# Out-projection of six feature blocks as fill of a scan's last stretch, and first feed-forward products in column halves

## The chip, the cores and the metric

The kernel runs on one core of one Trainium2 chip. The metric is the device time of one execution in microseconds. TensorE multiplies, VectorE (DVE), ScalarE (ACT) and GpSimd (POOL) do the rest, SyncE (SP) and POOL issue most transfers.

## The reference, cut to what matters

Two transformer blocks on 512 tokens of 1024 features, in float32. The first block's first layer is a bidirectional RWKV-7 mixer followed by a residual sum, a layer norm and a SwiGLU feed-forward of width 2816; a pooling layer with a mixture of experts and the second block (attention and a convolutional feed-forward) come behind and aren't touched.

```python
def rwkv7_out(y, feats, r_k, g1, g2, lnx_g, lnx_b, w_o):
    ...
    yn = ((y - mean) * lax.rsqrt(var + RK_GN_EPS)).reshape(b, n, D_MODEL) * lnx_g + lnx_b
    ...
    gate = jax.nn.sigmoid(xg @ g1) @ g2
    return ((yn + bonus).astype(xg.dtype) * gate) @ w_o
```

Behind it the layer computes, with alpha = 4 ** 0.25 and gates gt1, gt2 from the adaptive modulation, x = layer_norm(alpha * x + gt1 * y), then h = x * (1 + sc2) + sh2, then swiglu(h) = (silu(h @ w1) * (h @ w3)) @ w2.

## The kernel before

**Products in parts.** A float32 product is made of three: each operand is split into a high part (a cast on ACT, L167) and a low part (the difference on DVE, L168), and mm3 (L173) issues high x high, high x low and low x high into one accumulator.

**The scan (phase_rwkv).** Eight feature blocks f of 128 features (two heads each) go one after the other through 12 steps of 64 tokens, three chain() stretches of 16 slots each, so 48 slots per block and 384 in all. A step computes Rs (ACT, L863), UV (ACT, L871) and the state S (DVE, L890), with the decayed state SP by POOL (L850) beside it. weave() runs the chain with side work: the inverses of the next tiles, gram(), features of the block after, and tail(f - 1), which normalises a finished block, adds the bonus, multiplies by the gate and writes it to DRAM (ygd, L945). The copy of a block's result out of PSUM is L899: the end of its scan.

**Background work.** background() is one generator: the jobs of the k, r and v projections of pairs p = 1 to 3 (job(), matmuls at L979), then 40 yields of adaptive modulation (ada(), matmuls at L235). fill() calls it after each slot, by the table PACE of (slot, yields done by then); all that fill() issues stands behind the chain's last matmul. A lateral job loads its left operand in pieces of 1 MB on the POOL queue (L969, tile x, two buffers) and its weights on SP (tile w). In a v job a yield is six matmuls of 256 columns.

**The order of instructions.** A scheduler orders each engine's instructions when the program is built, by a model of time and by the order of the program; an instruction of a later stage can stand ahead of one of an earlier stage if its buffers are free. Engines then run their instructions in that order.

**Behind the scan (body).** After the last slot the rest of the background is run, then tail(7), then: the eight blocks of y are read back into xres and split into y3 (two of the three buffers of the pool act), x is loaded into xres, the whole w_o is loaded and split, and for each of four token blocks tb and two column halves 24 matmuls of 512 columns are issued, resid_add() adds to xres (DVE, L1311 and L1315), and norm_tail() normalises (statistics on DVE L1130, a power on POOL L1137, the scaling on ACT L1139) and turns the block into features (transposes on PE L1162, scale and shift on ACT L1169 and DVE L1171, the split into hT). hT has two parts, in the same pool act. Then phase_ffn(): glu() for each pair of w1 and w3 columns, beside ada_sum(), which computes the next modulations on DVE (L288) from weights that it loads on SP.

## Time and profile before

| | us |
|---|---|
| time before, median of 3 runs | 3043.56 (3039.95 to 3060.38) |
| the profiled execution's own time | 3043.58 |
| its span in the trace | 3041.8 |

In that execution TensorE was busy 2665.8 us (88%), DVE 1562.1, ACT 1218.2 and POOL 826.3. A busy TensorE is not TensorE at its peak: matmuls are pipelined and their ends are modelled. Busy time tells which engine could be the limit of a stretch; the waits in the timelines tell which one is. In the rows below, an idle time in brackets is that of the engine before the instruction, and behind the arrow stands what ended it.

### The profile page before, as it was taken

What the parts mean: (1) busy time and instruction counts of PE and PEld (TensorE: products, weight loads), DVE (VectorE), ACT (ScalarE), POOL (GpSimd) and SP (SyncE); (2) the same over time, 40 slices, a digit from 0 to 9 for tenths busy, and PEclk for the clock granted to TensorE, in tenths of its full rate; (3) what the DMA queues carried; (4) which work ended last, traced back from release to release, by engine and by line L of the source; (5) the groups of instructions that cost most, each with busy time, mean ns of one, the idle gap of its engine ahead of it and who ended that gap; (6) DMA issues with size and microseconds to landing.
All of it is one profiled execution on the core that took longest, in us unless ns stands there. A gap on an engine that the chain in (4) does not pass through costs nothing. (4 is left out here: it accounts for less than half of the span.)

```text
span 3041.8 us, 49004 instructions
## 1 busy us (share of the span) xinstructions
PE 2665.8 (88%) x19592; PEld 2127.8 (70%) x19592; DVE 1562.1 (51%) x2443; ACT 1218.2 (40%) x2267; POOL 826.3 (27%) x908
## 2 busy tenths in 40 slices
PE   5878788898898766899897999999949989989999
PEld 3666677677776545677686787887837855778887
DVE  5865656756656536754446531111155467554544
ACT  5644545555555423225432321111123367342422
POOL 2453434534534321018534300000033100112120
PEclk8976788997888778999898999999979979999999
DMA  7562334544543536757622767788972212122321
GB/s 256 184 219 68 97 114 144 183 137 129 172 135 105 173 128 199 242 173 229 194 84 97 267 208 236 256 273 291 299 253 72 71 37 72 58 83 89 106 88 65
DMA packets 346594, 477.99 MB, mean 157 GB/s; under 512 B 45842, under 2 KB 242723, under 8 KB 339703
## 3 DMA queue, kind: packets, MB, share of 16 engines
q1 hardware_dynamic: 328664, 404.80, 41.2%
q0 software_dynamic: 10480, 60.31, 6.1%
q10 hardware_dynamic: 7216, 9.68, 1.0%
q8 instruction: 157, 2.57, 0.4%
q14 instruction: 77, 0.63, 0.1%
HBM read 419.34 MB, written 55.39 MB: 156 GB/s over the span
## 5 line engine op out<-in xcount | busy, mean ns | idle before, releaser
L168 DVE TENSOR_TENSOR wl<-w,wh 128x1024 fp32r<-128x1024 f32 (+1 forms) x271 | 332.1, 1232 | 473.6 <-ACT wh L167 472.4
L167 ACT CAST wh<-w 128x1024 fp32r<-128x1024 f32 (+1 forms) x271 | 256.5, 953 | 551.3 <-PE mm L173 469.3
L173 PE MATMUL mm<-act,wh 128*128 128x512 f32 x1408 | 439.6, 394 | 14.5 <-ACT act L167 14.5
L173 PEld LDWEIGHTS mm<-act,wh 128*128 128x128 f32 x1408 | 265.6, 190 | 73.7 <-ACT act L167 15.0
L173 PE MATMUL mm<-act,wl 128*128 128x512 f32 x704 | 275.5, 391 | 0.0
L173 PE MATMUL mm<-wh,act 128*128 128x512 f32 x816 | 262.0, 400 | 7.5 <-ACT wh L167 4.2
L173 PEld LDWEIGHTS mm<-wh,act 128*128 128x128 f32 x816 | 157.3, 193 | 47.0 <-ACT wh L167 7.2
L286 POOL TENSOR_TENSOR act<-act 128x512 f32<-128x512 f32 x96 | 142.7, 1491 | 139.7 <-ACT act L285 75.5
L301 POOL DMA_DIRECT2D bc<-gate x6 | 3.6, 593 | 614.4 <-DVEq L1707 523.6
L173 PE MATMUL mm<-wl,act 128*128 128x512 f32 x408 | 163.1, 400 | 2.8 <-DVE wl L168 2.8
L1220 DVE TENSOR_TENSOR silu<-silu,mm 128x512 f32<-128x512 f32 (+4 forms) x77 | 35.3, 458 | 248.3 <-PE mm L1216 183.1
L173 PEld LDWEIGHTS mm<-act,wl 128*128 128x128 f32 x704 | 133.1, 189 | 28.1
L799 DVE STREAM_TRANSPOSE XT<-T 128x512 f16<-128x512 f16 x120 | 84.6, 705 | 100.4 <-ACT T L797 100.2
L743 POOL TENSOR_TENSOR GA<-GA,masks 128x512 f32<-128x512 f32 (+1 forms) x96 | 100.1, 1053 | 103.7 <-ACT GA L742 100.5
L739 PE MATMUL gm<-kr,bk 64*128 64x128 f32 (+1 forms) x768 | 115.4, 324 | 4.2 <-ACT GA L742 2.4
L739 PEld LDWEIGHTS gm<-kr,bk 64*128 64x128 f32 x768 | 99.4, 224 | 25.2 <-ACT GA L742 9.8
L792 DVE TENSOR_TENSOR W<-pW,masks 128x512 f16<-128x512 f32 x120 | 81.9, 682 | 64.4 <-PE pW L790 63.8
L850 POOL TENSOR_TENSOR SP<-S,pc 128x64 f32<-128x64 f32 x176 | 59.2, 355 | 194.3 <-DVE S L890 183.0
L1216 PEld LDWEIGHTS mm<-moxh,w 128*128 128x128 f32 x704 | 105.0, 190 | 8.3 <-issue 5.7
L1216 PE MATMUL mm<-moxh,w 128*128 128x192 f32 (+1 forms) x704 | 108.0, 314 | 2.5 <-DMA w<-in_moe_w_dram 2.4
L797 ACT CAST T<-pT 128x512 f16<-128x512 f32 x120 | 69.7, 581 | 83.2 <-PE pT L795 79.8
L285 ACT ACTIVATE act<-act,cT 128x512 f32<-128x512 f32 x96 | 67.6, 723 | 81.6 <-DMA act<-in_w_ada_dram 81.4
(521 smaller groups left out, 6382.7 us busy)
## 6 DMA issues: line engine op xcount, KB each, us to landing
w<-in_moe_w_dram SPq DMA_DIRECT2D x109, 1024.0 KB
w<-in_ffn_w_dram SPq DMA_DIRECT2D x32, 1024.0 KB
act<-in_ada_w_dram SPq DMA_DIRECT2D x96, 256.0 KB
act<-in_w_ada_dram SPq DMA_DIRECT2D x96, 256.0 KB
w<-in_w_up_dram SPq DMA_DIRECT2D x22, 1024.0 KB
x<-xdk POOLq DMA_DIRECT2D x18, 1024.0 KB, 5.6
x<-xdv POOLq DMA_DIRECT2D x18, 1024.0 KB, 5.7
w<-in_ada_w_dram SPq DMA_DIRECT2D x32, 512.0 KB
```

Of the source, the lines that this page charges most:

```text
L167: self.nc.scalar.copy(out=hi, in_=x)
L168: self.nc.vector.tensor_tensor(out=lo, in0=x, in1=hi.bitcast(F32), op=OP.subtract)
L173: self.nc.tensor.matmul(ps, x, y, start=start and i == 0, stop=stop and i == 2, skip_group_check=True)
L285: nc.scalar.activation(out=wt, in_=wt, func=AF.Copy, scale=c)
L286: nc.gpsimd.tensor_tensor(out=acc, in0=wt, in1=acc if kk else bias, op=OP.add)
L739: nc.tensor.matmul(pss[par][:, s2, d, :nc_], bkj(d, par, j), KR[d][PR(par), j::12, :][:, :nc_ // 64, :], start=True, stop=True)
L743: nc.gpsimd.tensor_tensor(out=out, in0=out, in1=gm, op=OP.mult)
L792: nc.vector.tensor_tensor(out=W16, in0=pW, in1=lmask[:, li, None].to_broadcast(sh), op=OP.mult)
L797: nc.scalar.copy(out=T16, in_=pT)
L799: nc.vector.transpose(fl(XT), fl(T16))
L850: nc.gpsimd.tensor_tensor(out=SP[:, d], in0=S[:, d], in1=PC[d][:, j:j + 1].to_broadcast([128, 64]), op=OP.mult)
L1216: nc.tensor.matmul(ps[:, :n], w[:, kk], xT[:, kk, :n], start=(kk == 0), stop=(kk == KB - 1))
```

## The change

- tail() splits its result and writes both parts to DRAM (yparts) in place of ygd; for f = 7 three operations go from POOL to DVE.
- A fourth kind of job, "o", for four column blocks p of 256 columns: it multiplies feature blocks 0 to 5 of y with the rows of w_o, 6 x 4 x 3 matmuls of 256 columns in 12 yields; o_out() multiplies by the gate, adds alpha * x and writes the sums to DRAM (ysums). The four jobs stand at the end of background().
- PACE: the modulation's 40 yields end at slot 322 and no longer at 384, and 26 yields of the new jobs follow up to slot 384; the rest runs four yields a step within tail(7).
- body: xres is loaded with the sums; y of blocks 6 and 7 is loaded as parts into one buffer of act; two weight tiles in place of eight; six matmuls of 512 columns for each tb and column half. norm() of block tb + 1 stands before turn() of block tb.
- glu() for the first pair: columns 0 to 255 of both products, then turn(3), then columns 256 to 511.

```diff
@@ -30,7 +30,7 @@
-        (220, 137), (236, 153), (252, 161), (268, 177), (384, 217))
+        (220, 137), (236, 153), (252, 161), (268, 177), (322, 217), (384, 243))
@@ -302,7 +302,7 @@
-def phase_rwkv(k, tables, tables2, modulate, yg):
+def phase_rwkv(k, tables, tables2, modulate, yo):
@@ -312,7 +312,8 @@
-    xd = {(n_, w): k.dr.tile([128, KB, 2, w], F32, name=f"xd{n_}{w}") for n_, w in (("k", NT), ("k", NCX), ("r", NT), ("v", NT), ("v", NCX))}
+    xd = {("o", NT): yo["parts"]}
+    xd.update({(n_, w): k.dr.tile([128, KB, 2, w], F32, name=f"xd{n_}{w}") for n_, w in (("k", NT), ("k", NCX), ("r", NT), ("v", NT), ("v", NCX))})
@@ -321,7 +322,7 @@
-    W = {"r": a["rk_w_rkv"][0, 0], "k": a["rk_w_rkv"][0, 1], "v": a["rk_w_rkv"][0, 2]}
+    W = {"r": a["rk_w_rkv"][0, 0], "k": a["rk_w_rkv"][0, 1], "v": a["rk_w_rkv"][0, 2], "o": a["rk_w_o"][0]}
@@ -363,7 +364,20 @@
-    OUT = {"k": k_out, "r": r_out, "v": v_out}
+    def o_out(p, pss, lat, pool, tag, *_):
+        g = k.t(pool, [128, 512], tag=tag)[:, :256]
+        nc.sync.dma_start(out=g, in_=k.gates["0"][0][:, p * 256:(p + 1) * 256].to_broadcast([128, 256]))
+        for i, ps in enumerate(pss):
+            t = k.t(pool, [128, 512], tag=tag)
+            rows = lambda x: x[i * 256:(i + 1) * 256, p * 256:(p + 1) * 256].rearrange("(b p) n -> p b n", p=128)
+            nc.sync.dma_start(out=halves(t), in_=rows(a["x"][0]))
+            nc.vector.tensor_tensor(out=halves(ps), in0=halves(ps), in1=g[:, None, :].to_broadcast([128, 2, 256]), op=OP.mult)
+            nc.vector.scalar_tensor_tensor(out=t, in0=t, scalar=ALPHA, in1=ps, op0=OP.mult, op1=OP.add)
+            nc.sync.dma_start(out=rows(yo["sums"]), in_=halves(t))
+        return
+    OUT = {"k": k_out, "r": r_out, "v": v_out, "o": o_out}
@@ -903,14 +917,15 @@
+            eng = nc.gpsimd if f < 7 else nc.vector
-            nc.gpsimd.tensor_tensor(out=vh, in0=vh, in1=st["cf"][:, :, None].to_broadcast([128, 8, 64]), op=OP.mult)
+            eng.tensor_tensor(out=vh, in0=vh, in1=st["cf"][:, :, None].to_broadcast([128, 8, 64]), op=OP.mult)
-            nc.gpsimd.tensor_tensor(out=y3, in0=y3, in1=mean[:, :, None].to_broadcast([128, 8, 64]), op=OP.subtract)
+            eng.tensor_tensor(out=y3, in0=y3, in1=mean[:, :, None].to_broadcast([128, 8, 64]), op=OP.subtract)
@@ -921,7 +936,7 @@
-            nc.gpsimd.tensor_tensor(out=y3, in0=y3, in1=rs[:, :, None].to_broadcast([128, 8, 64]), op=OP.mult)
+            eng.tensor_tensor(out=y3, in0=y3, in1=rs[:, :, None].to_broadcast([128, 8, 64]), op=OP.mult)
@@ -942,7 +957,11 @@
-            nc.sync.dma_start(out=yg[f], in_=yn)
+            hi, lo = (k.t(bst, [128, 512], F32R, tag="st") for _ in range(2))
+            k.part_to(hi, lo, yn)
+            for i, x in enumerate((hi, lo)):
+                nc.sync.dma_start(out=yo["parts"][:, f, i], in_=x.bitcast(F32))
+            made["y", f] = True
@@ -956,11 +975,13 @@
-            acc = [ps for ps in pss] if lat and n_ != "v" else [halves(ps)[:, i] for ps in pss for i in range(2)]
-            for kk in range(KB):
+            byrow, last_ = n_ in "vo", (6 if n_ == "o" else KB) - 1
+            acc = [ps for ps in pss] if lat and not byrow else [halves(ps)[:, i] for ps in pss for i in range(2)]
+            for kk in range(last_ + 1):
+                    n4 = min(4, last_ + 1 - kk)
-                    nc.sync.dma_start(out=raw, in_=W[n_][kk * 128:(kk + 4) * 128, p * 256:(p + 1) * 256].rearrange("(k p) n -> p k n", p=128))
+                    nc.sync.dma_start(out=raw[:, :n4], in_=W[n_][kk * 128:(kk + n4) * 128, p * 256:(p + 1) * 256].rearrange("(k p) n -> p k n", p=128))
@@ -969,15 +990,15 @@
-                    if n_ == "v":
+                    if byrow:
-                    st, sp_ = kk == 0 and (one or i % 2 == 0), kk == KB - 1 and (one or i % 2 == 1)
+                    st, sp_ = kk == 0 and (one or i % 2 == 0), kk == last_ and (one or i % 2 == 1)
-                    if i % 2 == 1 or (lat and n_ != "v"):
+                    if i % 2 == 1 or (lat and not byrow):
@@ -1024,6 +1045,9 @@
+            for p in range(4):
+                assert all(made.get(("y", f)) for f in range(6))
+                yield from job("o", p, True)
@@ -1068,8 +1092,11 @@
+        for _ in tail(7):
+            for _ in range(4):
+                next(mods, None)
-        run(tail(7))
@@ -1139,7 +1166,7 @@
-def norm_tail(k, sp, psp, tb, xres, gbc, bbc, hT, scol, bcol):
+def norm_rows(k, sp, tb, xres, gbc, bbc):
@@ -1147,8 +1174,7 @@
-    if hT is not None:
-        to_feature(k, sp, psp, xh, hT, slice(tb * 128, (tb + 1) * 128), scol, bcol)
+    return xh
@@ -1198,13 +1224,22 @@
-def glu(k, psp, sp, xT, n, w1, w3, g):
+def glu(k, psp, sp, xT, n, w1, w3, g, cols=None):
-        for w in (w1, w3):
+        if cols is not None and i == 0:
+            ws = [k.part(w[:, :, :128]) for w in (w1, w3)]
+            pss = [k.t(psp, [128, 512], tag="mm") for _ in ws]
+            for cs, make in cols:
+                make()
+                for w, ps in zip(ws, pss):
+                    for kk in range(KB):
+                        k.mm3(ps[:, cs], at(w, ALL, kk), at(xT, ALL, kk, cs), kk == 0 and cs.start == 0, kk == KB - 1 and cs.stop == n)
+        for w in (w1, w3) if not pss else ():
@@ -1257,7 +1292,7 @@
-def phase_ffn(k, hT, xres, gate2, psp, sp, gp, act, side):
+def phase_ffn(k, hT, xres, gate2, psp, sp, gp, act, side, cols):
@@ -1274,7 +1309,7 @@
-            glu(k, psp, sp, hT, NT, w1, w3, out)
+            glu(k, psp, sp, hT, NT, w1, w3, out, cols if f == 0 else None)
@@ -2067,8 +2102,8 @@
-        ygd = k.dr.tile([KB, 128, NT], F32, name="ygd")
-        phase_rwkv(k, tables, tables2, modulate, ygd)
+        yo = {"parts": k.dr.tile([128, KB, 2, NT], F32, name="yparts"), "sums": k.dr.tile([NT, D], F32, name="ysums")}
+        phase_rwkv(k, tables, tables2, modulate, yo)
@@ -2087,28 +2122,32 @@
-            with tc.tile_pool(reuse_waits="tile", name="wo3", bufs=5) as wo3:
-                y3 = feat()
-                yg = xres.rearrange("p t d -> p (t d)").rearrange("p (f n) -> p f n", f=KB)
-                for f in range(KB):
-                    nc.sync.dma_start(out=yg[:, f, :], in_=ygd[f])
-                for f in range(KB):
-                    k.part_to(*at(y3, ALL, f), yg[:, f, :])
-                nc.sync.dma_start(out=xres, in_=a["x"][0].rearrange("(t p) d -> p t d", p=128))
-                ws = []
-                for i in range(4):
-                    raw = k.load_w(a["rk_w_o"][0][(i % 2) * 512:(i % 2 + 1) * 512, (i // 2) * 512:(i // 2 + 1) * 512])
-                    ws += [k.part(raw[:, 2 * q:2 * q + 2, :], wo3 if len(ws) + q < 5 else k.wq) for q in range(2)]
-                hT = None
-                for tb in range(4):
-                    for hf in range(2):
-                        ps = k.t(psp, [128, 512], tag="mm")
-                        for kk in range(KB):
-                            k.mm3(ps, at(y3, ALL, kk, slice(tb * 128, (tb + 1) * 128)), at(ws[hf * 4 + kk // 2], ALL, kk % 2), kk == 0, kk == KB - 1)
-                        resid_add(k, sp, tb, hf, ps, gate, xres)
-                    hT = hT or feat()
-                    norm_tail(k, sp, psp, tb, xres, *gb, hT, *cols)
+            raw = k.load_w(a["rk_w_o"][0][768:1024, :])
+            ws = [k.part(raw[:, :, hf * 512:(hf + 1) * 512]) for hf in range(2)]
+            y67 = k.t(act, [128, 2, 2, NT], F32R, tag="act")
+            for i in range(2):
+                nc.gpsimd.dma_start(out=y67[:, i], in_=yo["parts"][:, 6 + i])
+            nc.sync.dma_start(out=xres, in_=yo["sums"].rearrange("(t p) d -> p t d", p=128))
+            hT = feat()
+            rows_ = {}
+            def norm(tb):
+                cs = slice(tb * 128, (tb + 1) * 128)
+                for hf in range(2):
+                    ps = k.t(psp, [128, 512], tag="mm")
+                    for i in range(2):
+                        k.mm3(ps, at((y67[:, i, 0], y67[:, i, 1]), ALL, cs), at(ws[hf], ALL, i), i == 0, i == 1)
+                    resid_add(k, sp, tb, hf, ps, gate, xres, None)
+                rows_[tb] = norm_rows(k, sp, tb, xres, *gb)
+            def turn(tb):
+                to_feature(k, sp, psp, rows_[tb], hT, slice(tb * 128, (tb + 1) * 128), *cols)
+            for tb in range(4):
+                norm(tb)
+                if tb:
+                    turn(tb - 1)
+            turns = [(slice(0, 256), lambda: None), (slice(256, 512), lambda: turn(3))]
@@ -2117,7 +2156,7 @@
-                block, room = phase_ffn(k, hT, xres, gate0, psp, sp, gp, act, side)
+                block, room = phase_ffn(k, hT, xres, gate0, psp, sp, gp, act, side, turns)
```

## Rows read from the trace of the kernel before

**Rows 1.** The page's first line: span and instructions.

```profile
span 3041.8 us, 49004 instructions
```

**Rows 2.** Stretches: length, busy (count) of PE, PEld, DVE, ACT, POOL; PEclk, DMA share, GB/s.

```profile
905.00:990.00 85.00, 73.82 (x1211) 54.86 (x1210) 51.44 (x91) 44.73 (x108) 39.83 (x62) 0.84 0.42 121
...
1068.50:1084.50 16.00, 5.10 (x14) 2.44 (x14) 3.77 (x7) 3.97 (x7) 4.93 (x5) 0.50 0.93 300
1084.50:1158.70 74.20, 55.56 (x216) 44.79 (x216) 23.99 (x43) 12.99 (x19) 17.19 (x15) 0.82 0.18 60
1158.70:1181.10 22.40, 2.04 (x10) 1.60 (x9) 21.82 (x36) 10.21 (x20) 9.27 (x9) 0.57 0.87 279
1181.10:1194.50 13.40, 13.40 (x49) 10.68 (x50) 10.08 (x14) 5.28 (x6) 0.00 (x0) 0.82 0.79 258
...
1070.00:1080.00 10.00, 3.83 (x13) 2.44 (x14) 1.62 (x4) 2.87 (x5) 4.93 (x5) 0.50 1.06 330
```

**Rows 3.** Timeline of ACT at the scan's end: start us, us, instruction.

```profile
1047.20 0.27 ACT L863 COPY Rs<-ch 128x128 f32<-128x128 f32 x1 [2.07 <-PE ch L833]
1050.75 0.27 ACT L863 COPY Rs<-ch 128x128 f32<-128x128 f32 x1 [2.07 <-PE ch L833]
...
1062.06 0.26 ACT L863 COPY Rs<-ch 128x128 f32<-128x128 f32 x1
1062.21 4.83 ACT L167 CAST wh<-w 128x1024 fp32r<-128x1024 f32 x5
1067.07 0.57 ACT L871 ACTIVATE UV<-ch 64x128 f32<-64x128 f32 x2
1068.41 0.59 ACT L899 COPY yc<-y 128x512 f32<-128x512 f32 x1 [0.78 <-PE y L833]
```

**Rows 4.** Timeline of SP's queue around the scan's end.

```profile
1043.05 2.31 SPq L155 DMA_DIRECT2D w<-in_rk_w_o_dram  x4
...
1092.11 0.38 SPq L2098 DMA_DIRECT2D xres<-in_x_dram  x1
```

**Rows 5.** Timeline of PE from the out-projection to the feed-forward.

```profile
1084.56 0.80 PE L173 MATMUL mm<-wh,act 128*128 128x512 f32 x1 [3.29 <-ACT act L167]
...
1107.08 1.97 PE L1162 MATMUL mm<-ctile,rsq 128*128 128x128 f32 x8 [8.54 <-ACT rsq L1139]
...
1181.07 2.17 PE L173 MATMUL mm<-act,wh 128*128 128x512 f32 x4 [8.57 <-ACT act L167]
```

**Rows 6.** Timeline of DVE in the same stretch.

```profile
1100.68 0.69 DVE L1315 SCALAR_TENSOR_TENSOR xres<-xres,silu 128x512 f32<-128x512 f32 x1 [4.37 <-DMA xres<-in_x_dram]
...
1158.55 1.29 DVE L168 TENSOR_TENSOR act<-u,act 128x512 fp32r<-128x512 f32 x2 [0.18 <-PE mm L173]
```

**Rows 7.** Groups by line (count, busy us, mean ns) of 1158.7 to 1181.1, then 1084.5 to 1158.7.

```profile
L288 DVE SCALAR_TENSOR_TENSOR act<-act,cT 128x512 f32<-128x512 f32 x11 | 11.4, 1044 | 0.4 <-DMA act<-in_ada_w_dram 0.4
...
L168 DVE TENSOR_TENSOR act<-xres,act 128x512 fp32r<-128x512 f32 x8 | 5.3, 692 | 4.8 <-DMA ygd<-yn 3.7 <-ACT act L167 1.0
```

**Rows 8.** Timeline of PE: a yield of a v job and its successor; a modulation yield.

```profile
737.43 0.50 PE L979 MATMUL bg<-x,wh 128*128 128x256 f32 x2
...
738.25 0.41 PE L790 MATMUL pW<-T,nl 128*128 128x64 f16 x8
...
1036.83 0.64 PE L235 MATMUL bg<-w,cT 128*32 128x256 f32 x8
```

**Rows 9.** Line L899, ends of the scans of heads 4, 5, 6 (ns, then start us).

```profile
L899 ACT COPY yc<-y x1: 587/587/587, 798.0 to 798.0; 128x512 f32<-128x512 f32 x1
L899 ACT COPY yc<-y x1: 567/567/567, 905.2 to 905.2; 128x512 f32<-128x512 f32 x1
L899 ACT COPY yc<-y x1: 591/591/591, 989.7 to 989.7; 128x512 f32<-128x512 f32 x1
```

**Rows 10.** DMA issues of 300 to 1060: count, KB each, median us to landing.

```profile
x<-xdv POOLq DMA_DIRECT2D x16, 1024.0 KB, 5.5
```

**Rows 11.** Waits of POOL in 560 to 870: us in total, times, longest.

```profile
POOL x L969 <- PE bg L979: 12.4, 7, 4.9
```

## Prediction

> **What bounds the kernel now.** I read the page's span first [rows 1]: 3041.8 us. The times list the same profiled execution at 3043.58 us, and the median of the runs shown is 3043.56, so a change summed on the trace carries over to the median one to one. Then I read the table by stretches [rows 2] around the place of the diff. In the scan's stretch 905 to 990 TensorE is busy 73.8 of 85.0 us: nearly full. From the end of the scan it is not: busy 5.1 of 16.0 us in the last head's tail, 55.6 of 74.2 in the out-projection, 2.0 of 22.4 between that and the feed-forward. The first feed-forward pair of products ends at 1194.5.
>
> The timelines say what each gap waits for. Head 7's scan ends with the copy at 1068.41 [rows 3]. Its last step but one took 1050.75 to 1062.06, where the step before it took 3.55 us, and from its Rs to its UV passed 5.0 us. ScalarE stood in order behind casts of out-projection weights (five of them, 4.83 us, sit between Rs and UV); their loads had been issued at 1043.05 [rows 4]. So some 12 us of the scan's end are a wait for weights of the next stage. Out-projection starts at 1084.56 and the feed-forward at 1181.07 [rows 5]: 96.5 us for 192 products of 512 columns, with four waits for a normalised block. The reader should see why the last wait is long: the first low part of the normalised activations is written at 1158.55, right after the last product [rows 6]. It needs a buffer that the y parts hold until then, so the turning of all four blocks piles up behind it; and in that pile VectorE is busy 21.8 of 22.4 us [rows 2], 11.4 of them with eleven instructions of the next layer's modulation [rows 7].
>
> **The change, part by part.** *Out-projection out of the row.* Six of eight feature blocks leave the serial stretch; 48 of 192 products stay. That frees the buffer: y of two blocks takes one buffer, both parts of the activations have one from the start, and turning of block n can follow the norm of n+1. This is what the change can win; what follows is what it pays.
>
> *Fill in the scan.* A job of the new kind has 12 yields of six 256-column products, four jobs have 48. By the pacing table, background work stands at 217 yields after slot 384 before and at 243 after, 40 of them adaptive-modulation yields both times (now squeezed into slots 268 to 322). So 26 yields are added under heads 5, 6 and 7. Their price: a value job has the same six products, and one such yield goes from 737.43 to 738.25 [rows 8], 0.82 us at the full clock; an adaptive yield takes 0.64. From below it can be nothing: 11 us of TensorE in 905 to 990 are idle [rows 2]. From above: head 5 (about 29.5 yields by the table) took 798.0 to 905.2, head 6 (16.5) 905.2 to 989.7 [rows 9], 22.7 us for 13 yields, 1.75 us each; this holds head 7's features too, so it is a bound. 26 yields cost 0 to 46 us. I take 20, near the TensorE price (26 x 0.82 = 21): the engine is nearly full there, and the squeezed modulation yields carry neither splits nor POOL-issued loads. The splits of y move from after the scan into the tails: eight were 5.3 us of VectorE [rows 7]; seven now lie beside other heads, 1 us on the path, 0 to 5.
>
> *The stall at the end.* Eight weight tiles to split become two before the feed-forward's, and 4 MB of load become 1 MB. Of the 12 us I count 10 as gone (0 to 12): the scheduler can still put feed-forward casts early. Scan end: 1068.4 + 20 + 1 - 10 = 1079.4.
>
> *From the scan's end to the sums.* Of 48 yields about 27 are done, 21 left, woven four to a step into the tail of head 7. 21 x 0.82 = 17 us, and head 7's tail (the stretch of 16.0 us) lies under them. That tail's three operations moved from POOL to VectorE are hidden there too; without that cover they could give or take 1 us. Between jobs, the second half's row tile must wait for the gate tile's buffer (two buffers, three tiles): multiply, load of x, add, before the next job has its second accumulator. I take 4 us; bounds 0 and 7 (a 1 MB load lands in 5.5 us [rows 10], and this one is a quarter of it). After the last product: two multiplies, the load, the add, the write of the sums, 8 us (5 to 13, by the same row twice at the top). Then xres is read back in one 2 MB load: that of x was issued at 1092.11 [rows 4] and its first reader ran at 1100.68 [rows 6], 9 us. 17 + 4 + 8 + 9 = 38 us; the sums are in place at 1117.4. The 48 remaining products need only the y parts of the tail, which ends before, so they are hidden under this wait. On SP's queue the stores of sums wait for VectorE, and behind them stand the last tail's loads and its stores of parts; a delay of these by the 8 us would still be inside the wait for the sums.
>
> *From the sums to the end of the first pair.* Here VectorE sets the pace. In 1084.5 to 1181.1 it was busy 24.0 + 21.8 = 45.8 us [rows 2]; less 11.4 (modulation) and 5.3 (splits of y) [rows 7], 29 us are the four blocks with the first weight splits. Behind its last norm stand POOL, ScalarE and the transposes, of which some 3 us show: from 1100.68 to the transposes at 1107.08 one block needed 6.4 us [rows 5, 6]. Then the second column half: 48 products of 256 columns at a sixth of 0.82 us (weight load for each included, as in that row), 7 us; the first half runs before, under the last block's norm. Modulation will again sit between: I take 5 of the 11.4. 29 + 3 + 7 + 5 = 44, bounds 37 and 51. End of the pair: 1161.4, against 1194.5.
>
> The sum: 33.1 us earlier, and the rest of the kernel is the same work behind it: 3043.6 - 33.1 = 3010.5 us.
>
> **A rule that speaks against it.** The new jobs read y parts back through the POOL queue, 3 MB a job. The stretch 1070 to 1080 moved 330 GB/s at a DMA share of 1.06 [rows 2], and nothing in the trace is faster there. The Trainium skill (DMA: Bandwidth & Descriptors, Issuing engines are not separate DMA queues) says that queues issued from different engines run on the same 16 DMA engines and interleave. By that rule the re-reads and the feed-forward weights share one rate, which the trace's share of 1.06 agrees with, and the time would be that of the second rival below.
>
> **The rivals.** *Fill lands on the chain* (chance 0.15): each of the 26 yields costs the 1.75 us of the head difference. The scan's end is 46 - 20 = 26 us later, time 3037. For it: job yields bring splits on ScalarE and VectorE, the chain's own engines. Against: 13 yields' difference also holds a whole head's features.
>
> *The end is bound by DMA* (0.14): between the scan's end and the sums must move x parts 5, x rows and sums 2, y parts 1.5, out-projection and job weights 2, feed-forward weights 3, broadcasts 1.5, xres 2 MB (sizes from shapes, estimates as to what is left by then): 17 MB at 330 GB/s are 52 us instead of 38, time 3025. For it: the share of 1.06. Against: two tiles are loaded ahead and the weights may be loaded before, as the out-projection's were.
>
> *Slower: POOL's queue holds the chain* (0.06). Loads of parts are issued by POOL in order and wait for a buffer; the state's decay product L850 that each chain step needs is queued behind them. Before, POOL waited 12.4 us in 7 such waits, the longest 4.9 [rows 11], in heads with slack. If each of the 12 loads holds for 4.9 us what the path needs (the seven under heads 6 and 7 the decay product, the five after them the tail's power on POOL, L923), that is 59 us, time 3010.5 + 59 = 3069.5; slower begins at 2.8 us a load. Against: the wait's mean was 1.8 us, so 21 us and still a gain is the more likely form.
>
> *Better* (0.15): the tail's yields are not tied to the chain and drop into its gaps; nothing is left at the scan's end but the last job's output, and fill costs half. 10 us less in the scan and 10 less behind it: 2990.
>
> **How the numbers follow.** The forecast has 0.50, with its own range 2996 to 3026 (10 us of fill and 10 behind the scan either way). Faster or slower by 1% (30.4 us: under 3013, over 3074) is about what a measurement of this kernel can tell from no change. Under 3013 lie some 0.30 of the forecast's 0.50, the better case, and a tenth of the others: 0.48. Over 3074 lies at most half of the slower rival and mishaps of pacing: 0.06. Within 1%: 0.46. The range 2985 to 3045 leaves out the upper half of the slower rival, the top of the fill rival and the lower part of the better case, together under 2 in 10.
>
> **What would show it.** After: the scan's last copy near 1079 (1068 or less: fill free; 1100 and more: fill on the chain); no long step between the last Rs copies; head 7's tail with TensorE busy and at the full clock, where before 0.50 was granted [rows 2]; xres ready about 38 us behind (50 and DMA share near 1: the DMA rival); POOL waits at the load of parts short; first feed-forward product some 25 us after xres (three of four blocks of the 29 us, and 3). I am wrong if head 6 or 7 grows by over 25 us, or if VectorE blocks after xres on modulation loads for over 15 us.

## The result, and the profile after

The changed kernel takes 3065.84 us (median of 18 runs, 3047.6 to 3074.28) beside 3041.74 for the kernel before on the same chip: the ratio is 1.0076, 95% interval 1.0062 to 1.0089. The forecast was 3010.5 us, a ratio of 0.989, within 2985 to 3045 us; the time lies above that range. The profiled execution took 3058.1 us.

The page's first line, to set beside [rows 1]:

```profile
span 3056.3 us, 49525 instructions
```

Some words stand for marks in the traces. "After" is the changed kernel, and "head n" is the scan of feature block n, from the end of the block before to its own copy out of PSUM. The first sum in xres is resid_add()'s first addition on VectorE. The first silu on ScalarE marks the end of the first feed-forward pair's products, and each pair leaves one cast of its gated product, gh; the 21st gh cast serves as a late mark.

The stretches of after, cut where the sum was cut: head 6, head 7, from the scan's end to the first sum in xres, from there to the first silu, and what follows. Columns as in [rows 2].

```profile
916.30:1013.00 96.70, 88.51 (x1339) 64.41 (x1338) 60.84 (x103) 46.96 (x111) 44.08 (x66) 0.86 0.55 167
1013.00:1092.40 79.40, 64.37 (x987) 53.11 (x986) 39.54 (x77) 34.71 (x85) 22.24 (x45) 0.87 0.70 226
1092.40:1152.80 60.40, 31.63 (x149) 27.56 (x150) 14.40 (x24) 6.44 (x11) 7.06 (x11) 0.72 0.61 204
1152.80:1218.50 65.70, 30.57 (x165) 27.47 (x164) 55.60 (x81) 22.25 (x35) 28.48 (x24) 0.69 0.47 148
1218.50:1545.00 326.50, 292.09 (x1282) 235.63 (x1281) 179.84 (x218) 128.65 (x173) 123.51 (x84) 0.94 0.65 208
```

| term of the sum, us | forecast | after | difference |
|---|---|---|---|
| scan's end | 1079.4 | 1092.4 | +13.0 |
| from there to the sums in xres | 38 | 60.4 | +22.4 |
| from there to the end of the first pair | 44 | 65.7 | +21.7 |
| from there to the end of the span (before: 3041.8 - 1193.5 = 1848.3) | 1848.3 | 1837.8 | -10.5 |

The first three make 57.1 us. Less 10.5, and with 1.0 added because the prediction took the end of the pair before as 1194.5 where this cut has 1193.5, that is the 47.6 by which the span of 3056.3 misses 3008.7. The fourth is no gain that I can name: from the 21st gh cast of the feed-forward to the end, that stretch takes 1468 to 1479 us in before, after and the kernels below (e12 aside), 1467.8 in after.

The second row is the surprise. Neither TensorE (31.63 of 60.40 us) nor VectorE (14.40) is busy in it, and the DMA share is 0.61 at 204 GB/s, so the second rival's bound (the 330 GB/s of [rows 2]) doesn't account for it either. The timeline of the last tail's result, block 7's y, on its way to the out-projection:

```profile
1108.59 0.69 DVE L959 TENSOR_TENSOR yn<-yn,gm 128x512 f32<-128x512 f32 x1 [0.45 <-PE gm L958]
...
1131.13 0.62 ACT L167 CAST st<-yn 128x512 fp32r<-128x512 f32 x1 [14.41 <-DMA ysums<-st]
...
1136.23 0.69 DVE L168 TENSOR_TENSOR st<-yn,st 128x512 fp32r<-128x512 f32 x1 [3.84 <-DMA ysums<-st]
...
1136.96 0.33 SPq L963 DMA_DIRECT2D yparts<-st  x1
...
1145.22 0.54 POOL L2130 DMA_DIRECT2D act<-yparts  x1 [24.47 <-DMA yparts<-st]
...
1149.19 0.79 PE L173 MATMUL mm<-wh,act 128*128 128x512 f32 x1 [13.41 <-DMA act<-yparts]
```

The value is ready at 1109.3, and its high part is written 22 us later. What released the cast is the landing of a store of *sums* (ysums) out of a tile called st. The tail takes the tiles for its two parts from the pool that the jobs use, which has two buffers, and each new job takes three there: gate rows, x rows, x rows. The parts queue behind the jobs' stores and loads; the store of the parts, their load back by POOL and the products follow one after another.

### The profile page after: what moved, and what is told of

Read it like the earlier page. It is cut to its first block, busy times and chain, and to the rows that moved or that the text cites. A ratio compares the mean times of both kernels' runs of the same rounds, so it can differ in the third digit from the quotient of the medians.

```text
span 3056.3 us, 49525 instructions
## 1 busy us (share of the span) xinstructions
PE 2668.5 (87%) x19784; PEld 2136.1 (70%) x19784; DVE 1581.8 (52%) x2468; ACT 1219.1 (40%) x2273; POOL 844.0 (28%) x919
## 5 line engine op out<-in xcount | busy, mean ns | idle before, releaser
L168 DVE TENSOR_TENSOR wl<-w,wh 128x1024 fp32r<-128x1024 f32 (+1 forms) x277 | 333.3, 1209 | 490.2 <-ACT wh L167 488.8
L173 PE MATMUL mm<-act,wh 128*128 128x512 f32 (+1 forms) x1440 | 444.0, 391 | 18.8 <-ACT act L167 15.0
L173 PEld LDWEIGHTS mm<-act,wh 128*128 128x128 f32 x1440 | 271.9, 192 | 76.3 <-ACT act L167 15.4
L173 PE MATMUL mm<-act,wl 128*128 128x512 f32 (+1 forms) x720 | 279.4, 388 | 0.0
L173 PE MATMUL mm<-wh,act 128*128 128x512 f32 x720 | 231.0, 400 | 22.0 <-DMA act<-yparts 17.7
L173 PEld LDWEIGHTS mm<-wh,act 128*128 128x128 f32 x720 | 138.5, 193 | 56.3 <-DMA act<-yparts 18.5
L173 PE MATMUL mm<-wl,act 128*128 128x512 f32 x360 | 143.7, 400 | 3.0 <-DVE wl L168 2.9
L1000 PE MATMUL bg<-wh,x 128*128 128x256 f32 x480 | 129.2, 338 | 13.0 <-DMA x<-yparts 13.0
L864 POOL TENSOR_TENSOR SP<-S,pc 128x64 f32<-128x64 f32 x176 | 66.7, 396 | 202.2 <-DVE S L904 192.4
L1251 PEld LDWEIGHTS mm<-moxh,w 128*128 128x128 f32 x704 | 105.0, 190 | 7.3 <-issue 6.3
L1000 PEld LDWEIGHTS bg<-wh,x 128*128 128x128 f32 x480 | 95.0, 223 | 21.5 <-issue 8.9
```

Of the source, the lines that this page charges most:

```text
L168: self.nc.vector.tensor_tensor(out=lo, in0=x, in1=hi.bitcast(F32), op=OP.subtract)
L173: self.nc.tensor.matmul(ps, x, y, start=start and i == 0, stop=stop and i == 2, skip_group_check=True)
L864: nc.gpsimd.tensor_tensor(out=SP[:, d], in0=S[:, d], in1=PC[d][:, j:j + 1].to_broadcast([128, 64]), op=OP.mult)
L1000: m = nc.tensor.matmul(o, y, z, start=st and q == 0, stop=sp_ and q == 2, skip_group_check=True)
L1251: nc.tensor.matmul(ps[:, :n], w[:, kk], xT[:, kk, :n], start=(kk == 0), stop=(kk == KB - 1))
```

## The experiments

Ratios are against the kernel before, measured on the same chip; a run's milestones come from its own profiled execution. How far these scatter is seen in e7, e9, e11, e13 and e16, which differ only behind the scan: head 0 ends at 338.5 to 351.7 us, head 5 takes 110.1 to 117.0, head 6 100.0 to 105.0, head 7 80.3 to 87.0. So I compare lengths of heads and distances behind the scan's end, not absolute times. Each version has one trace, and a head's length that differs by less than this scatter shows nothing.

**e1: the parts in buffers of their own.**

```diff
-            hi, lo = (k.t(bst, [128, 512], F32R, tag="st") for _ in range(2))
+            hi, lo = (k.t(tp1, [128, 512], F32R, tag=t_) for t_ in ("vtok", "yc"))
```

> The two parts that each tail writes get buffers of their own kind (those of vtok and yc, which the same tail has done with) in place of the two that the jobs' rows and gates also use. Theory 'buffers': in the changed kernel the cast of the last tail's result waited 14.4 us for a store of sums, from 1109.3 to 1131.1, and heads 3 to 5 grew by 11 us with the same waits; so the last parts leave near 1110, the second load of y parts no longer starts at 1145, and heads 3 to 5 go back: 8 to 18 us faster than the changed kernel (3048 to 3058). Rival 'fill': the loss is the new jobs' work itself on the chain, whatever buffer the parts lie in: within 3 us of the changed kernel.

3044.68 us, ratio 1.0017 (1.0001 to 1.0034): about 0.6%, 18 us, of the loss is this. The same timeline:

```profile
1108.19 0.69 DVE L959 TENSOR_TENSOR yn<-yn,gm 128x512 f32<-128x512 f32 x1
...
1108.96 0.62 ACT L167 CAST vtok<-yn 128x512 fp32r<-128x512 f32 x1 [2.45 <-issue]
...
1111.04 0.69 DVE L168 TENSOR_TENSOR yc<-yn,vtok 128x512 fp32r<-128x512 f32 x1
...
1126.67 0.50 PE L173 MATMUL mm<-wh,act 128*128 128x512 f32 x1 [1.68 <-DMA act<-yparts]
```

The cast follows the result at once. Now the products stand behind the last product of the new jobs (1124.7), the first sum waits 8.6 us for the load of xres, and it comes 48.6 us behind the scan's end in place of 60.4. Head 3 is back too: 108.0 us, against 117.9 in after and 108.0 before; tails inside the scan had queued for the same two buffers. But the scan as a whole isn't shorter: heads 1 to 7 take 748.8 us in e1, 741.2 in after and 718.1 before, since every other head is longer in e1 than in after, by 1 to 5 us.

**e5: the gate rows in a buffer of their own as well.**

```diff
-        g = k.t(pool, [128, 512], tag=tag)[:, :256]
+        g = k.t(tp1, [128, 256], tag="ast")
```

> As the run with own buffers for the tails' parts, and the gate tile of a new job lies in the buffer of the modulation's rows (done by then), so that the job's two row tiles no longer wait for it. If the bubble between jobs that I put at 4 us, and the load of the second half's rows after the last product, are on the path: 3 to 8 us faster than the run with own buffers alone (3037 to 3042). If the loads of y parts set the pace behind the scan, the bubble lies under them: within 3 us.

3035.99 us, ratio 0.9994 (0.9964 to 1.0024). The first sum comes 41.0 us behind the scan's end, 7.6 less than in e1. Not all of that is the wait for the gate tile: 96 matmuls of the new jobs (16.0 yields) are left behind the scan's end, where after and e1 have 113 (18.8). The times of e1 and e5 alone don't part them, the intervals overlap. The stretch from the scan's end to the first sum is now nearer to the transfers' rate than in after (0.61, 204 GB/s):

```profile
1088.10:1129.10 41.00, 25.73 (x134) 22.19 (x134) 13.63 (x22) 5.17 (x10) 6.21 (x10) 0.79 0.82 283
```

**e2: no new product paced under the scan** (all 48 yields stand behind the last slot; in the trace 3.5 of them still begin before the scan's last copy).

```diff
-        (220, 137), (236, 153), (252, 161), (268, 177), (322, 217), (384, 243))
+        (220, 137), (236, 153), (252, 161), (268, 177), (384, 217))
```

> The pacing table of the kernel before: the modulation spread to slot 384 again, no new job paced under the scan, all 48 yields after it. Theory 'fill': the scan's end goes back from 1092 to 1070 to 1076, and the 26 yields behind it cost about as much again (1.3 to 1.8 us a yield, since each piece of 1 MB is waited for): total -5 to +20 us against the changed kernel. Theory 'buffers': the scan keeps 10 us of its growth (heads 3 to 5 have no new job): its end at 1078 or later.

3099.41 us, ratio 1.0168 (1.0128 to 1.0209). The scan's end came at 1109.2, not at the 1070 to 1076 of the theory 'fill'; head 6 alone took 111.0 us, which e14 takes up. Behind the scan a yield costs 75.8 / 44.5 = 1.7 us; in after it is 33.4 us for 18.8 yields, 1.8. The sum had 0.82. **e12** asks whether the loads of parts set that, with one load per job in place of three:

```diff
-                if kk % nq == 0:
+                if kk % nq == 0 and (n_ != "o" or kk == 0):
```

> The kernel e2_pace_before (all 48 yields of the products behind the scan, 76 us for them) with one load of the blocks' parts per product in place of three, the same tile being used three times; this leaves out two thirds of the parts. Theory (the 1 MB loads through two buffers set the 1.6 us per yield): last product 40 to 50 us behind the scan's end, time 3065 to 3075 against 3099. Rival (the clock and the matmuls' own work set it): over 65 us behind the scan's end, time 3088 to 3100.

The same stretch, from the scan's end to the last product, in e2 and then in e12:

```profile
1109.20:1185.00 75.80, 47.82 (x281) 45.18 (x282) 19.81 (x32) 10.13 (x17) 10.25 (x17) 0.80 0.74 248
```

```profile
1090.90:1141.60 50.70, 36.87 (x282) 35.26 (x283) 19.61 (x32) 10.23 (x17) 5.92 (x9) 0.97 0.56 175
```

With two of three loads gone, the same products take 50.7 us, 1.1 per yield, just above the upper end of what the theory of the loads had expected: 14 of the 25 us are waiting, and 11 are TensorE's own, at a granted clock of 0.97 in place of 0.80. (e12's total, 4973 us, says nothing of this: its loss lies behind the 21st gh cast, 3373 us to the end where the others take 1468 to 1479, and why was not looked into.) The waits of e2 in this stretch, total, times, longest:

```profile
POOL x L990 <- PE bg L1000: 56.0, 9, 12.3
...
PE bg L1000 <- DMA x<-yparts: 22.6, 7, 4.7
```

A load waits for a buffer that TensorE still reads, and TensorE then waits for the load's landing, 5.5 us by [rows 10]. But the loads are not all of it. e14, below, has the pace of e2 and tiles of their own for parts and gate rows, and the same stretch takes 61.0 us, 1.4 per yield:

```profile
1085.80:1146.80 61.00, 44.21 (x282) 42.08 (x282) 19.98 (x32) 10.11 (x17) 10.26 (x17) 0.83 0.87 290
```

So some 15 us of e2's 75.8 go with the two shared buffers. Whether the remaining waits for loads come of the number of buffers or of the rate of the transfers, 290 GB/s at a share of 0.87 here, e12 doesn't tell, since it takes the transfers away as well. **e6** tries finer pieces (e5 with four buffers of half the size):

```diff
-    bx = PB("bxB", 2)
+    bx = PB("bxB", 4)
...
-            nq = 2 if lat else 4
+            nq = 1 if lat else 2
```

> As the run before it, with the jobs' left operand in pieces of half the size and four buffers in place of two (the same room). Theory 'loads behind the scan': 17 to 18 yields took 33 us there, TensorE waiting for parts four times, since a buffer is asked for only when the one before it is used up; with finer pieces the next ones are on the way earlier: the last new product 5 to 10 us nearer to the scan's end, 5 to 10 us faster in all. Rival 'rate': the engines of the transfers are the limit there (17 MB), and pieces change nothing: within 3 us; the more issues on POOL may cost the scan some us.

3038.46 us, ratio 1.0009 (0.9985 to 1.0033): the last product stands 22.2 us behind the scan's end and no longer 25.7, but the first sum 40.4 behind it, as in e5 (41.0). Nothing is won in the time, and the rival 'rate' is not excluded: from the scan's end to the first sum the transfers run at a share of 0.87 and 297 GB/s.

**e7: all 48 yields under the scan** (e5 with one number changed).

```diff
-        ... (322, 217), (384, 243))
+        ... (322, 217), (384, 265))
```

> Own buffers as in the first of these three, and all 48 yields paced under heads 6 and 7 (265 by slot 384). Theory 'loads behind the scan': in the scan a yield costs about 0.9 us (24 us of growth for 26), behind it 1.9; 21 yields moved under the chain lengthen the scan by 15 to 22 us and leave the tail alone behind it (16 us in place of 33), so within 6 us of the first of the three. Theory 'fill on the chain' (1.75 us a yield): 15 us slower or more.

3029.88 us, ratio 0.9974 (0.9949 to 0.9998). The last new product now comes before the last product of the scan:

```profile
1091.13 0.28 PE L1000 MATMUL bg<-wh,x 128*128 128x256 f32 x1
1091.34 0.45 PE L847 MATMUL y<-UV,GA 128*64 128x64 f32 x8
```

and within the scatter the scan has not become longer by it, where the theory had 15 to 22 us: heads 1 to 7 take 748.1 us, in e9, e11, e13 and e16, with the same scan, 740.8 to 752.2, and in e5, e6 and c4, with 22 yields fewer under it, 741.3 to 756.0. The first sum comes 31.1 us behind the scan's end.

**e9: the load of xres behind the last store of parts** (e7 with that order; in e7 the load of 2 MB was issued 1.4 us ahead of the first of these stores).

```diff
...
+            with tc.issue_after(yo["last"].ins):
-            nc.sync.dma_start(out=xres, in_=yo["sums"].rearrange("(t p) d -> p t d", p=128))
+                nc.sync.dma_start(out=xres, in_=yo["sums"].rearrange("(t p) d -> p t d", p=128))
```

> The kernel with own buffers and all products under the scan, and the load of xres (2 MB) put on SyncE behind the last store of block 7's parts. In the version without that order the load was issued at 1104.1, ahead of those stores (1105.5, 1106.2), which landed by 1115.5; the first out-projection product stood at 1119. Theory (the parts' stores stand behind the load): the first product 4 to 8 us earlier, ratio 0.994 to 0.996 against the kernel before. Rival (the load of xres ends last whatever its place): first xres sum at 1123 as before, ratio 0.997 to 0.999.

3032.13 us, ratio 0.9979 (0.995 to 1.0008), the rival's. The first sum comes 28.0 us behind the scan's end, 3.1 earlier than in e7, and block 7's products 3.0 earlier, for which 4 to 8 were expected; the first silu, 91.1 behind it, is no earlier than in e7 (91.5). A miss: the next stretch takes it back.

**What lengthens heads 6 and 7: e10, e14, e15.** e10 is the kernel before with its modulation squeezed as in the changed one and nothing else:

```diff
-        ... (268, 177), (384, 217))
+        ... (268, 177), (322, 217), (384, 217))
```

> The kernel before with one number changed: its modulation work, spread over slots 268 to 384 of the scan, is put into slots 268 to 322, as in the changed kernel; nothing else. Theory (the growth of head 6 by 12 to 17 us comes from the squeezed modulation): head 6 is 95 us or more against 84.6, the scan ends no earlier than 1075, time 3042 to 3056. Rival (it comes from the new products, the parts or their buffers): head 6 stays at 84 to 88, the scan ends at 1060 to 1070, time 3030 to 3044.

3041.56 us, ratio 1.0002 (0.9987 to 1.0017). Head 6 takes 94.7 us against 84.6, head 7 76.0 against 78.7, just short of the theory's 95 and 3042 us: 7.4 us more for both, and the scan's end 8.1 later, but no loss in the time that the runs would show. e14 is the opposite: own buffers as in e5, the pace table of e2.

> The changed kernel with buffers of its own for parts and gate tile, and with the pace table of before (modulation over slots 268 to 384, all 48 yields of the new products behind the scan). Theory (squeezed modulation and the new products under the scan lengthen heads 6 and 7, the storing of parts does not): head 6 84 to 89 us, the scan ends at 1066 to 1074, the last product 70 to 78 us behind it, time 3060 to 3080. Rival (the tails' parts lengthen the heads too): head 6 95 us or more, the scan ends at 1080 or later, time 3075 to 3095.

3066.59 us, ratio 1.0093 (1.0063 to 1.0123), and a miss of my theory: head 6 takes 106.0 us, with no squeezed modulation and no new product in it, and the scan ends at 1085.8. Both are what the rival had (the tails' parts lengthen the heads), though its time of 3075 or more did not come; the last product stands 61.0 us behind the scan's end, not the 70 to 78 expected. Head 6 in e10 and in e14 (for before, [rows 2] has nearly the same stretch; cut at its ends it is 84.5 us, 73.52 busy, x1207, clock 0.84):

```profile
905.80:1000.50 94.70, 85.90 (x1294) 61.35 (x1295) 56.40 (x97) 45.18 (x107) 41.69 (x61) 0.81 0.42 125
```

```profile
903.20:1009.20 106.00, 92.11 (x1207) 69.15 (x1210) 53.01 (x92) 45.51 (x109) 39.85 (x62) 0.68 0.35 100
```

Two different causes. In e10, and in after with 1339 matmuls at 0.86, the clock is much as before and TensorE has more to do (87 and 132 matmuls, 12.4 and 15.0 us of its time). In e14 it is the same 1207 matmuls as before, in 18.6 us more of TensorE's time, at a granted clock of 0.68; e2 and e12, with the same pace, show 0.65 and 0.68 there. Most of it lies in one stretch near the head's end, first e14, then the like stretch of before:

```profile
975.00:1006.00 31.00, 31.00 (x325) 23.43 (x325) 6.49 (x14) 9.10 (x21) 6.16 (x10) 0.50 0.18 53
```

```profile
967.00:987.00 20.00, 19.00 (x345) 14.19 (x346) 7.70 (x17) 8.88 (x21) 6.50 (x12) 1.00 0.29 85
```

TensorE is busy throughout, at half the clock. Within the scan e14 differs from before in what the tails do and in the order that the scheduler made of it. Why the clock falls there is not settled, and nothing here varies it alone.

e15 spreads the modulation to slot 340 and puts the new products into 340 to 384:

> The kernel e13_gain_later with modulation over slots 268 to 340 in place of 268 to 322 and the new products in 340 to 384. Theory (head 6 is longer because TensorE has more in it than fits): head 6 shorter by 5 to 8 us, head 7 longer by 2 to 5, the scan's end 2 to 4 us earlier, and as much off the time. Rival (the same work only moves between the heads): the scan's end within 1.5 us of that of e13_gain_later.

3042.7 us, ratio 1.0006 (0.9983 to 1.0029). Both expectations failed: head 6 took 90.2 us, 9.8 less than e13's, but head 7 97.7, 17.4 more, the scan's end came 23.7 us later than in e13, and the last product ran 13.5 us behind it. The yields crowded into head 7 cost more than those taken out of head 6 gave back.

**The stretch behind the sums: e3, e4, c4, e11, e13, e16.** e3 holds the next layer's modulation on VectorE until the blocks are turned:

```diff
+                    with tc.issue_after(k.hold.ins) if f == 0 else nullcontext():
-                    next(side, None)
+                        next(side, None)
```

> The first three steps of the next layer's modulation are put behind the last split of the turned blocks on VectorE (order only). Theory 'pile': 24.7 us of modulation on VectorE lie between 1150 and 1217, among the norms and turns of the four blocks; held back, the first pair of products ends 10 to 18 us earlier and the modulation is done under the feed-forward, where VectorE is half idle: 8 to 16 us faster than the changed kernel. Rival: TensorE waits there for the POOL and ScalarE steps of each norm, or the feed-forward then waits for the modulation: within 4 us.

3063.28 us, ratio 1.0066 (1.004 to 1.0093). The first silu comes 51.7 us behind the first sum in place of 65.7, and the gain is given back: at the 21st gh cast e3 is 5 us ahead of after, and at the end of the span 1.2. So the time is the rival's, within 4 us of after. From the first silu to the 21st gh cast e3 takes 9.4 us more; TensorE waits 19.3 us there for the modulation in place of 16.4, and the larger part, 7.5 us, is its own busy time (343.1 in place of 335.6), which no run explains. **c4** joins the same hold to e6:

> The second of these three with the modulation held behind the last turn on VectorE as well. Held back alone it won 14.5 us up to the first pair's end in the profile and gave 9 to 10 of them back within the next eight pairs: 0 to 6 us faster than without the hold. If it is faster than 3030 us, it beats the kernel before by more than the measurement's uncertainty.

3044.44 us, ratio 1.0022 (0.9995 to 1.0048), not apart from e6. **e4** takes the column halves away (turn(3) before the first pair, no cols):

> The last block is turned before the first pair, and the pair's products take all 512 columns at once, as before. Both theories: the first half of the columns (about 7 us of products) no longer runs under the last block's norm, so 3 to 7 us slower than the changed kernel; if the halves cost as much as they hide (twice as many weight loads, a clock at half), within 2 us.

3069.53 us, ratio 1.0084 (1.0058 to 1.011), not apart from the 1.0076 of the changed kernel. The first silu comes 65.0 us behind the first sum, in after 65.7: no gain of the halves shows.

What remains in the stretch shows in VectorE's timeline of after, and POOL's beside it:

```profile
1164.72 0.68 DVE L1346 TENSOR_TENSOR silu<-mm,bc 128x512 f32<-128x512 f32 x1
1165.32 2.55 DVE L168 TENSOR_TENSOR act<-u,act 128x512 fp32r<-128x512 f32 x1
1167.80 2.85 DVE L1348 TENSOR_TENSOR xres<-xres,silu 128x512 f32<-128x512 f32 x1
1170.57 0.68 DVE L168 TENSOR_TENSOR act<-u,act 128x512 fp32r<-128x512 f32 x1
```

```profile
1164.94 2.38 POOL L1175 TENSOR_TENSOR xres<-rsq,bg 128x1024 f32<-128x1024 f32 x1
1167.40 2.69 POOL L1176 TENSOR_TENSOR xres<-xres,bb 128x1024 f32<-128x1024 f32 x1
```

VectorE instructions of 0.68 us take 2.55 and 2.85 while a gain or bias of the normalised residual runs on GpSimd, and end some 0.55 us behind it. **e11** is e9 without these eight operations:

```diff
-    nc.gpsimd.tensor_tensor(out=z, in0=xh, in1=gbc, op=OP.mult)
-    nc.gpsimd.tensor_tensor(out=z, in0=z, in1=bbc, op=OP.add)
```

> The kernel e9_sums_behind_parts without the eight operations on GpSimd that multiply the normed residual by its gain and add its bias behind the out-projection; this leaves out the gain and bias in the residual. Theory (these stretch VectorE's work on the path, 0.94 against 0.69 us for the residual's multiply and 0.91 against 0.68 us for the low parts): from the first sum in xres to the first silu 48 to 54 us against 60 to 66, 8 to 12 us off the time of e9. Rival (the chain of the turns itself and modulation on VectorE set it): less than 4 us off.

3021.83 us, ratio 0.9941 (0.9925 to 0.9958), and 50.4 us from the first sum to the first silu against 63.1 in e9, as the theory had it. The theory's two groups give 3.9 us of this (L168 7.3 to 5.5, the residual's add 7.5 to 5.4); the larger part of VectorE's time, 6.6 us with two instructions fewer, is in the modulation, which also reads two tiles in SBUF. In e9, 20 of these take 0.70 to 0.75 us and three, beside the gain or bias, 2.31 to 2.73; in e11 all 21 take 0.75 at most. The groups in e9 and then in e11:

```profile
L288 DVE SCALAR_TENSOR_TENSOR act<-act,cT 128x512 f32<-128x512 f32 x23 | 22.1, 969 | 7.5 <-DMA act<-in_ada_w_dram 7.3
```

```profile
L288 DVE SCALAR_TENSOR_TENSOR act<-act,cT 128x512 f32<-128x512 f32 x21 | 15.5, 748 | 5.5 <-DMA act<-in_ada_w_dram 5.3
```

But e11 leaves work out. **e13** was to run it later, behind the last low part in the order of issue, with the normalised rows kept in xres:

```diff
+    for tb in range(4):
+        z = xres[:, tb, :]
+        with tc.issue_after(k.split.ins):
+            k.nc.gpsimd.tensor_tensor(out=z, in0=z, in1=gbc, op=OP.mult)
+            k.nc.gpsimd.tensor_tensor(out=z, in0=z, in1=bbc, op=OP.add)
```

> The kernel e9_sums_behind_parts with the normed residual kept in place and its gain and bias applied by GpSimd behind the last turn, in place of between the turns: all of the computation is there. Theory (what e11_no_gain won, 13 us to the first silu, came from GpSimd and VectorE working at once on the path, and it stays won when the eight operations run under the feed-forward): first silu at 1168 to 1172, ratio 0.993 to 0.995 against the kernel before. Rival (it is given back under the feed-forward, as with the modulation held back): first silu at 1168 to 1172 but the seventh pair no earlier than before, ratio 0.997 to 0.999.

3034.75 us, ratio 0.998 (0.9957 to 1.0003), with the first silu 65.3 us behind the first sum, which neither side had expected. POOL's timeline tells why: the edit did not move the work.

```profile
1121.22 2.39 POOL L1182 TENSOR_TENSOR xres<-xres,bg 128x1024 f32<-128x1024 f32 x1 [1.73 <-ACT u L1201]
...
1154.87 2.67 POOL L1183 TENSOR_TENSOR xres<-xres,bb 128x1024 f32<-128x1024 f32 x1
```

**e16** ties it down by data: gbc is made to depend on the last low part (plus that value minus itself).

```diff
+    h = hT[1][:, KB - 1, NT - 1:NT].bitcast(F32)
+    nc.gpsimd.tensor_tensor(out=o, in0=h, in1=h, op=OP.subtract)
+    nc.gpsimd.tensor_tensor(out=gbc[:, 0:1], in0=gbc[:, 0:1], in1=o, op=OP.add)
```

> As e13_gain_later was meant: there the eight operations still ran at 1121 to 1157 us, between the turns, with the stretch to the first silu at 65 us; here they read a value that the last turn makes, so that they can't begin before it. Theory (GpSimd and VectorE working at once on the path cost the 13 us that e11_no_gain won): from the first sum in xres to the first silu 48 to 54 us against 63 in e9_sums_behind_parts, the low parts on VectorE back at 0.69 us; of it at least 6 us is left at the end, ratio 0.993 to 0.996. Rival (given back under the feed-forward): same stretch, ratio 0.997 to 0.999. Rival (e11 was faster for another reason): the stretch stays at 60 us or more.

3026.78 us, ratio 0.9971 (0.9949 to 0.9993). VectorE's groups from the first sum to the first silu, after and then e16:

```profile
L288 DVE SCALAR_TENSOR_TENSOR act<-act,cT 128x512 f32<-128x512 f32 x23 | 24.7, 1076 | 4.8 <-DMA act<-in_ada_w_dram 4.5
L1348 DVE TENSOR_TENSOR xres<-xres,silu 128x512 f32<-128x512 f32 x8 | 7.4, 938 | 0.0
L168 DVE TENSOR_TENSOR act<-u,act 128x512 fp32r<-128x512 f32 x8 | 7.3, 913 | 0.0
...
L1346 DVE TENSOR_TENSOR silu<-mm,bc 128x512 f32<-128x512 f32 x7 | 4.7, 676 | 0.6 <-PE mm L173 0.6
```

```profile
L288 DVE SCALAR_TENSOR_TENSOR act<-act,cT 128x512 f32<-128x512 f32 x21 | 21.7, 1041 | 2.7 <-DMA act<-in_ada_w_dram 2.5
...
L168 DVE TENSOR_TENSOR act<-u,act 128x512 fp32r<-128x512 f32 x8 | 5.3, 681 | 0.2 <-ACT act L167 0.2
L1358 DVE TENSOR_TENSOR xres<-xres,silu 128x512 f32<-128x512 f32 x8 | 5.3, 668 | 0.0
```

The stretch is 52.1 us against 63.1 in e9, and L168 and the residual's add are back at their short times: GpSimd beside VectorE cost 11 us here. (The modulation's mean is still 1041 ns because of its last three instructions, 2.78 to 2.91 us each, which run beside GpSimd's work from 1178 on; the 18 ahead of them take 0.73 to 0.75.) Most of the gain is given back. From the first silu to the first gh cast pass 14.1 us in e16 and 2.7 in e9, while GpSimd does the eight operations (22.4 us from 1177.99); TensorE waits 8.8 us for a low part of weights on VectorE. Counted from the first sum to the 21st gh cast, 3.3 us of the 11 are left (428.3 against 431.5). So the rival was right on the time: its 0.9971 is not apart from the 0.9979 of e9.

No version that does all of the work is faster than before by 1%. e7 and e16 come nearest, by 0.3%, with intervals that just exclude 1.

## Why the prediction was wrong, point by point

**Scan's end, +24 us where the sum had +11.** The stall of weights at the end is gone, as forecast: head 7's last steps take 6.7 and 4.2 us, with no step like the one of 11.3 [rows 3]; yet head 7 is no shorter (79.4 us against 78.7). The 26 yields were priced at 20 us; e7 against e5 shows 22 more at nothing that exceeds the scatter. (By the pace table head 5 holds 28.9 yields, not 29.5, so the bound from the heads is 1.8 us a yield; nothing hangs on it.) The squeezed modulation was priced at nothing; in e10 it makes head 6 longer by 10 us, with TensorE busy 85.9 of its 94.7, and the scan by 8. Head 3 grew by 10 from the tails' shared buffers, which e1, e5 and e7 undo, but their scans are not shorter for it. Heads 1 to 7 take 718.1 us before, 741.2 in after, 748.8, 741.3 and 748.1 in e1, e5 and e7, and still 743.5 in e14, where neither new products nor squeezed modulation lie under the scan. All but the first write parts in the tails, for which the sum had 1 us on the path, 0 to 5. So that term, or the order of instructions that comes with it, cost far more than 1 us at least in e14, where 21 of the 25 us lie in head 6 with its lower clock; what makes the scan of after longer is not isolated. No single head grew by the 25 us that I had named as proof against me.

**From the scan's end to the sums, 60.4 in place of 38.** This is the step that failed. The sentence was: "a delay of these by the 8 us would still be inside the wait for the sums". I had seen the clash of gate and row tiles (two buffers, three tiles) and priced it at 4 us, and had the stores of parts in SP's queue, but I did not ask from which pool the tail takes its parts. It is the same one: parts were held 22 us, not 8, and then the products that need them, not the sums, came last (the load of xres was issued at 1136.17, and no sum waited for it; block 7's products began at 1149.19). With own parts (e1) the stretch is 48.6 and the first sum does wait for the load of xres, 8.6 us; with the gate tile apart (e5) it is 41.0: 19.4 of the 22.4 us. The clash priced at 4 us measured 7.6, the 2.8 yields fewer behind the scan included. In the time, these two edits take the ratio from 1.0076 to 0.9994, 0.8% of the 1.9% by which the forecast of 0.989 missed.

**The yield behind the scan** is a mis-sized term: 0.82 us from a v job's yield [rows 8], inside the scan, where other work covers the wait for the loads; 1.8 us bare in after, 1.6 in e5 and 1.4 in e14, where the shared buffers are out of the way. The 17 us for 21 yields became 33.4 for 18.8. It was hidden by the larger wait in after, and it bounds e1 and e5.

**From the sums to the end of the first pair, 65.7 in place of 44.** I let 5 us of modulation into the stretch and there were 24.7 (23 instructions of L288). VectorE waited 4.5 us for its loads, below the 15 that I had named, so neither of my two signs of being wrong showed what was wrong. The other term is a kind that the sum did not have: VectorE's own instructions grow when GpSimd runs beside them. The groups show which ones: L168 and L1348 read both operands from tiles in SBUF and go from 0.68 to a mean of 0.91 and 0.94 us, and L288 has a mean of 0.97 in e9 and 0.75 in e11, while L1346, whose first operand is an accumulator of TensorE, stays at 0.676. The Trainium skill (SBUF — State Buffer, SBUF: two separate sides) says that a VectorE operation with two inputs in SBUF and a GpSimd operation that reads SBUF hold a shared port exclusively, each for the whole instruction; this trace agrees, with 2.55 us beside a GpSimd instruction of 2.38, of which the last 0.55 follow its end. Holding modulation back (e3) or moving GpSimd's work (e16) shortens the stretch by 14 and 11 us, but 9 and 8 of these are lost again up to the 21st gh cast, so this term cost the kernel far less than it cost the stretch.

**The rivals.** POOL's queue did not hold the chain: under heads 6 and 7 it waited 7.8 us in all for the loads' buffers, 3.1 at the longest, and the last tail's power ran at 1097.01, released by VectorE. That this rival's 3069.5 us lies near the measured time is luck. The end of after was not bound by DMA, with a share of 0.61 and 204 GB/s; waits for buffers and landings decided. With the buffers apart the share is 0.82 (e5) and 0.87 (e6), so there this rival is not excluded. Fill did not land on the chain at 1.75 us a yield (e7). "Better" had one true point: yields do drop into the chain's gaps (e7). None of the rivals was the slower case that came.

## What to carry to other kernels

When a step moves into another stage, write down for each tile that it takes the pool, the number of buffers and who else holds them until when; a store out of a tile holds its buffer until it lands, so a result can queue behind transfers that it has nothing to do with. Price work that runs bare by its loads' landing times and not by its price inside a busy stage, and ask whether the busy stage still has room for it before leaving it behind. A stretch shortened by putting work off is a gain only if the next stage has room on the engine that gets it; follow one milestone two stages on before believing it.

## What the runs showed of the hardware that I had not expected

- VectorE instructions of 0.68 us took 2.55 and 2.85 us beside GpSimd instructions of 2.38 and 2.69 and ended some 0.55 us behind them; with these moved (e16), the eight low parts averaged 0.681.
- The same 1207 matmuls of head 6 took 73.5 us of TensorE's time at a granted clock of 0.84 (before) and 92.1 at 0.68 (e14), 21 us in the length of the head. In e14 TensorE was busy for 31.0 us on end (975 to 1006) at a granted clock of 0.50. What brought the lower clock stays open.
- Two of three loads of 1 MB left out took 25 of 76 us off 44.5 yields (e2 against e12), 11 of them in TensorE's own busy time, at a granted clock of 0.97 in place of 0.80.
